# A two-layer hybrid trunk in fp32 on one core: pinned casts of operands, double-width buffers for sums of weights, and norms' sums two blocks later

## The chip, the cores and the metric

The kernel runs on one core of a Trainium2 chip. The metric is the device time of one execution, in microseconds (us). The kernel before took 2816.06, 2812.41 and 2814.46 us in three runs, a median of 2814.46 us. In the trace, PE is the matmul engine (TensorE), DVE is VectorE, ACT is ScalarE, POOL is GpSimd and SP is the engine that issues most of the DMAs; POOL issues the rest.

## The reference

The reference is one inference step of a model with two layers. 1024 prompt positions and 8 single samples share the weights; the width is 1024, the MLP's inner width 4096, and everything is float32. Cut to what matters here:

```python
for l in range(2):
    sh1, s1, g1, sh2, s2, g2 = split(silu(c) @ ada_w[l] + ada_b[l])   # adaLN
    h = rmsnorm(x, norm_mix[l]) * (1 + s1) + sh1
    out = even_mixer(h) if l == 0 else mamba_mixer(h)     # each with its own states
    x = x + g1 * out
    h = rmsnorm(x, norm_mlp[l]) * (1 + s2) + sh2
    x = x + g2 * (square(relu(h @ mlp_w1[l])) @ mlp_w2[l])
y = rmsnorm(x, norm_final)
```

The outputs are y for prompt and samples and the mixers' new states.

## The kernel before

**Layout and matmuls.** x stands transposed on the chip, as 8 tiles of 128 rows (channels) by 1032 columns (1024 prompt positions and 8 samples). A float32 product is made of three matmuls in PE's fast 32-bit format: each operand is cast to a high part on ACT, the low part is the difference to it on DVE, and `mm3` (L484, L487, L488) adds hi·hi, hi·lo and lo·hi. So each unit of weights (128x1024, 512 KB) costs one ACT cast to whi and one DVE subtraction to wlo. whi and wlo have three buffers each, so the cast for a unit waits until PE is through with the unit three before.

**The two MLPs.** Each is done by Strassen's scheme with seven products. The first projection (units "a") runs over 16 pairs of tiles (`AOPS`); `operand` makes the sums of weights there, `kept` fetches back tiles that were written out, `ff_out` applies the activation and stores the sums of activations in DRAM (td). The second projection (units "b", 64 of them in `BOPS`, eight for each of the passes i = 0 to 5 and sixteen half-size ones for i = 6) multiplies weights by operands rr, loaded back from td by POOL's queue in `load_op` (four DMAs of 516 KB for each half operand) and split into a high and a low part by `parts` (ACT's cast L836, DVE's subtraction L837); `split_op` says after which unit a part is split. Passes 2 to 5 need sums of two weights: `prep` loads one summand into h (two tiles of 512 columns, t2 and t3), the other into raw, adds or subtracts them on DVE (L448, L450, L452), casts (L453) and subtracts (L454). The sums of passes 2 and 3 are stored to DRAM (sd) and are the summands of later passes. Passes 0, 1 and 6 use plain weights (L463, L464). `need` prepares three units ahead of PE (AHEAD = 3).

**What runs beside.** While MLP 0's second projection runs, `ada_gen` streams layer 1's adaLN weights in the same loop, four DMAs of 256 KB for a unit into buffers from the same two rings (t2, t3), and PE multiplies them (L316). In the last two passes the norm of the next stage is made in steps, one step after each unit: `to_odd` after MLP 0, `to_out` after MLP 1. Squares are made on ACT (L548, L551) and added on DVE (L552), one matmul with ones sums over the partitions (L520, in `rms`, called by `rstd`); `sample_rstd` does the same for the samples (squares L599, matmuls L602). In the odd mixer `odd_dt` makes decays, writes them to DRAM and reads them back, spread over partitions (o.cd, o.dts).

**What sets the order.** Tiles and their semaphores are placed by a scheduler, which reorders each engine's instructions by its own estimate, except where the kernel keeps an instruction in program order with `tc.keep_in_program_order`. At run time every engine, and SP's DMA queue, takes its instructions in the order written down. SP waits, before it issues a DMA, for the one that it issued eight earlier to land, and for the buffer to be free.

Two lines that the change is about, of `parts` and of `prep`:

```python
S.copy(hi[:, c:c + 2], src)                 # L836: the scheduler places it
h = [t2(512), t3(512)]                      # two tiles, two DMAs, two adds, casts, subtractions
```

Of the kernel before, what the change touches and what calls it, by code (L numbers as in the profile page):

```python
# [32 lines left out]
N2, N3E, N3O, N3M = 8, 14, 6, 8  # L33
# [128 lines left out]
def kernel(ctx: ExitStack, tc: tile.TileContext, A: dict):  # L162
# [29 lines left out]
    def t3(w=W2, dt=F32):  # L192
        t = ph.pool.tile([P, W2], dt, name="t3", tag="t3", bufs=ph.n3)
        return t[:, :w]

# [187 lines left out]
    def operand(l, p, q):  # L383
# [3 lines left out]
        if key not in asrc:  # L387
# [7 lines left out]
            r[5], r[6] = t3(512), t3(512)  # L395
# [4 lines left out]
        if q in (7, 3):  # L400
            a11, a12, a21, s2 = r["a"]
            r[q] = t3(512)
            V.tensor_add(r[q], *((a11, a21) if q == 7 else (a12, s2)))
        return r.pop(q)

    def prep(kind, idx, raw=None, into=None):
# [20 lines left out]
        if kind[0] == "b":  # L427
# [3 lines left out]
            while sums and sums[0][0] <= idx - 2:  # L431
                _, d, h = sums.pop(0)
                for j in range(2):
                    dma(d[:, 512 * j:512 * j + 512], h[j])
            pr = BPROD[i]
            if pr in (5, 6, 7, 3):
# [4 lines left out]
                h = [t2(512), t3(512)]  # L441
                for j in range(2):
                    dma(h[j], a[:, 512 * j:512 * j + 512])
                raw = load_unit(*second)
                for j in range(2):
                    c = slice(512 * j, 512 * j + 512)
                    if pr == 5:
                        V.tensor_add(h[j], h[j], raw[:, c])  # L448
                    elif pr == 3:
                        V.tensor_sub(h[j], raw[:, c], h[j])  # L450
                    else:
                        V.tensor_sub(h[j], h[j], raw[:, c])  # L452
                    S.copy(hi[:, c], h[j])  # L453
                    V.tensor_sub(lo[:, c], h[j], hi[:, c].bitcast(F32))  # L454
# [140 lines left out]
    def sample_rstd(r):  # L595

        q = sm(KT * NS)
        for k in FOURS:
            S.activation(q.rearrange("p (k b) -> p k b", b=NS)[:, k], x[:, k, 512:520], AF.Square)  # L599
        pt = psm()  # L600
        for m in range(KT):
            PE.matmul(pt[:, :NS], ones, q[:, m * NS:m * NS + NS], start=m == 0, stop=m == KT - 1)  # L602
        return newton([(0, NS, pt)], NS, D, r)
# [174 lines left out]
    def mlp(l, gi, finish, more=None):  # L778
# [5 lines left out]
        saved, keep, U, B = {}, {}, {}, {}  # L784
# [41 lines left out]
        def load_op(i, kh):  # L826

            pool, tag = ((big, M["tags"][0]), (ph.pool, "hr"), (big, M["tags"][1]))[BSET[i][kh]]
            hi, lo = R[i, kh] = [pool.tile([P, KT, HX], F32R, name="rr", tag=tag, bufs=2, padded_shape=[P, KT, 520])
                                 for _ in range(2)]  # L830
# [18 lines left out]
        def kept(p):  # L849

            if p in SPLIT and p not in saved:
                saved[p] = t3(HX)
# [3 lines left out]
        for i, (p, q) in enumerate(AOPS):  # L856
# [55 lines left out]
            elif p >= 13 and q in (6, 4):  # L912
# [15 lines left out]
        for n, (i, hb, q, mp) in enumerate(BOPS):  # L928
# [33 lines left out]
            if i == 0:  # L962
                split_op((2, 2, 2, 2, 0, 1, 2, 1)[j])
            else:
                split_op((0, 0, 1, 1, 1, 1, 0, 1)[j] if i == 1 else (2, 1, 1, 1, 1, 1, 0, 1)[j] if i < 6 else (2, 1, 0, 0, 0, 0, 0, 0)[j] if hb == 0 else 0)
# [1133 lines left out]
```

## Time and profile before

| | |
|---|---|
| median of three runs | 2814.46 us |
| the profiled execution | 2808.36 us, its span 2806.4 us |
| PE busy | 2656.0 us, 95% of the span |
| DVE, ACT, POOL busy | 1995.5, 1495.9, 287.5 us |
| moved by DMA | 525.66 MB, 187 GB/s on average |

The stages follow each other: even mixer to 545 us, MLP 0's first projection to 892, its second to 1260, odd mixer to 2102, MLP 1's first projection to 2442, its second to the end. PE is busy nearly all the time, so the profile is read for the places where PE waits: in a list of PE's waits each row has the engine and line that PE waited for, the total, the number of times and the longest. In a timeline, the bracket behind a row gives how long the engine stood idle just before it and what ended that. PE's clock has its own column: 1.00 is 2.4 GHz, 0.50 is 1.2 GHz.

### The profile page before, as it was taken

What the parts mean: (1) busy time and instruction counts of PE and PEld (TensorE: products, weight loads), DVE (VectorE), ACT (ScalarE), POOL (GpSimd) and SP (SyncE); (2) the same over time, 40 slices, a digit from 0 to 9 for tenths busy, and PEclk for the clock granted to TensorE, in tenths of its full rate; (3) what the DMA queues carried; (4) which work ended last, traced back from release to release, by engine and by line L of the source; (5) the groups of instructions that cost most, each with busy time, mean ns of one, the idle gap of its engine ahead of it and who ended that gap; (6) DMA issues with size and microseconds to landing.
All of it is one profiled execution on the core that took longest, in us unless ns stands there. A gap on an engine that the chain in (4) does not pass through costs nothing. (4 is left out here: it accounts for less than half of the span.)

```text
span 2806.4 us, 49697 instructions
## 1 busy us (share of the span) xinstructions
PE 2656.0 (95%) x19442; PEld 2446.8 (87%) x19442; DVE 1995.5 (71%) x3796; ACT 1495.9 (53%) x2473; POOL 287.5 (10%) x492
## 2 busy tenths in 40 slices
PE   6999999999999998999899999999999999999897
PEld 4889888899999887989799897787779999999897
DVE  5666544787757566865799888998778776667766
ACT  5785511463444322446687766878756444444243
POOL 0000000023223111000000000000001322311010
PEclk8999999999999999999899999999999999999999
DMA  8232333256558899834554645543434655879754
GB/s 300 66 105 75 105 107 121 80 183 240 172 196 295 307 375 391 315 128 111 140 163 139 176 142 138 152 130 110 117 118 158 222 182 183 298 290 361 275 173 154
DMA packets 216923, 525.66 MB, mean 187 GB/s; under 512 B 38320, under 2 KB 56112, under 8 KB 216688
## 3 DMA queue, kind: packets, MB, share of 16 engines
q1 hardware_dynamic: 168304, 355.25, 39.7%
q0 software_dynamic: 48384, 167.23, 16.4%
q8 instruction: 153, 2.51, 0.4%
q14 instruction: 82, 0.67, 0.1%
HBM read 408.59 MB, written 113.80 MB: 186 GB/s over the span
## 5 line engine op out<-in xcount | busy, mean ns | idle before, releaser
L484 PE MATMUL pg<-hh,whi 128*128 128x256 f32 (+2 forms) x1616 | 536.7, 332 | 11.0 <-ACT hh L586 5.7
L487 PE MATMUL pg<-hl,whi 128*128 128x256 f32 (+2 forms) x1616 | 524.2, 324 | 1.9 <-DVE hl L587 1.9
L488 PE MATMUL pg<-hh,wlo 128*128 128x256 f32 (+2 forms) x1616 | 523.6, 324 | 0.0
L484 PE MATMUL pd<-rr,whi 128*128 128x258 f32 x1792 | 515.2, 288 | 8.3 <-DVE racc L960 7.2
L488 PE MATMUL pd<-rr,wlo 128*128 128x258 f32 x1792 | 511.2, 285 | 12.3 <-DVE wlo L454 10.5
L487 PE MATMUL pd<-rr,whi 128*128 128x258 f32 x1792 | 510.4, 285 | 0.0
L464 DVE TENSOR_TENSOR wlo<-raw,whi 128x1024 fp32r<-128x1024 f32 x222 | 271.0, 1222 | 199.7 <-ACT whi L463 193.2
L463 ACT CAST whi<-raw 128x1024 fp32r<-128x1024 f32 x222 | 231.4, 1044 | 326.8 <-PE pg L487 203.0
L484 PEld LDWEIGHTS pd<-rr,whi 128*128 128x128 f32 x1792 | 343.4, 192 | 28.2 <-issue 21.7
L488 PEld LDWEIGHTS pd<-rr,wlo 128*128 128x128 f32 x1792 | 343.2, 191 | 15.7 <-DVE wlo L454 11.5
L484 PEld LDWEIGHTS pg<-hh,whi 128*128 128x128 f32 x1616 | 309.1, 191 | 48.0 <-issue 8.7
L487 PEld LDWEIGHTS pd<-rr,whi 128*128 128x128 f32 x1792 | 343.3, 192 | 0.5 <-issue 0.5
L487 PEld LDWEIGHTS pg<-hl,whi 128*128 128x128 f32 x1616 | 309.0, 191 | 30.7 <-issue 5.2
L488 PEld LDWEIGHTS pg<-hh,wlo 128*128 128x128 f32 x1616 | 308.7, 191 | 24.2 <-issue 0.4
L484 PE MATMUL pd<-hh,whi 128*128 128x258 f32 x1024 | 294.2, 288 | 24.2 <-ACT whi L424 10.4
L487 PE MATMUL pd<-hh,whi 128*128 128x258 f32 x1024 | 292.3, 285 | 0.8 <-DVE hh L688 0.8
L488 PE MATMUL pd<-hh,wlo 128*128 128x258 f32 x1024 | 290.6, 284 | 0.0
L484 PEld LDWEIGHTS pd<-hh,whi 128*128 128x128 f32 x1024 | 196.3, 192 | 27.9 <-issue 11.3
L836 ACT CAST rr<-rr 128x1032 fp32r<-128x1032 f32 x112 | 117.8, 1057 | 155.1 <-DMA rr<-td 154.8
L487 PEld LDWEIGHTS pd<-hh,whi 128*128 128x128 f32 x1024 | 196.0, 191 | 1.9 <-DVE hh L688 1.4
L488 PEld LDWEIGHTS pd<-hh,wlo 128*128 128x128 f32 x1024 | 196.1, 192 | 0.0
L837 DVE TENSOR_TENSOR rr<-rr 128x1032 fp32r<-128x1032 f32 x112 | 136.0, 1229 | 65.3 <-ACT rr L836 64.7
(335 smaller groups left out, 5850.4 us busy)
## 6 DMA issues: line engine op xcount, KB each, us to landing
raw<-W SPq DMA_DIRECT2D x375, 512.0 KB, 4.3
td<-x POOLq DMA_DIRECT2D x224, 258.0 KB, 3.9
rr<-td POOLq DMA_DIRECT2D x112, 516.0 KB, 8.4
t<-ada SPq DMA_DIRECT2D x192, 256.0 KB, 5.8
t<-W SPq DMA_DIRECT2D x64, 256.0 KB, 6.6
sd<-t SPq DMA_DIRECT2D x64, 256.0 KB, 5.7
t<-sd SPq DMA_DIRECT2D x64, 256.0 KB, 5.9
t<-csd SPq DMA_DIRECT2D x64, 256.0 KB, 4.6
```

The costliest lines, as they stand in the source:

```text
L463: S.copy(hi, raw)
L464: V.tensor_sub(lo, raw, hi.bitcast(F32))
L484: mm = PE.matmul(pt, wh, xh, start=first and i == 0, stop=False)
L487: PE.matmul(pt, wh, xl, start=False, stop=False)
L488: PE.matmul(pt, wl, xh, start=False, stop=last and i == n - 1)
L836: S.copy(hi[:, c:c + 2], src)
L837: V.tensor_sub(lo[:, c:c + 2], src, hi[:, c:c + 2].bitcast(F32))
```

## The change

Four things change.

1. A ring of four double-width buffers, t6 (2 x 524 columns), takes the place of t3 (eight of 524) in the MLP phases. `operand` and `kept` put two tiles into one; in `prep` h is one tile of 1024 columns: one DMA of 512 KB where there were two of 256 KB, one sum, one cast (L456 of the changed kernel), one subtraction (L457). The adaLN weights use halves of t6 as well.
2. The casts of the operands (L836, now L840) are pinned in ACT's order, and read and write contiguous memory. The table in `split_op`'s calls is changed: the first operand's parts are split during pair 14, not from pair 13 on, and passes 0 and 1 split at other units.
3. `to_odd` and `to_out` make the norm's matmul two steps after the last squares; `sample_rstd` is a generator whose matmuls come two steps after its squares.
4. In `odd_dt` the sample decays are stored so that the four loads of o.dts read rows of 512 bytes, and these loads and that of o.cd move one step later.

```diff
@@ prep
-                h = [t2(512), t3(512)]
-                for j in range(2):
-                    dma(h[j], a[:, 512 * j:512 * j + 512])
+                h = t6()[:, 0:1024]
+                dma(h, a)
                 raw = load_unit(*second)
...
+                S.copy(hi, h)
+                V.tensor_sub(lo, h, hi.bitcast(F32))
@@ sample_rstd
-        q = sm(KT * NS)
+        q = tp.tile([P, KT * NS], F32, name="sq8", tag="racc", bufs=2)
         for k in FOURS:
             S.activation(q.rearrange("p (k b) -> p k b", b=NS)[:, k], x[:, k, 512:520], AF.Square)
+        yield
         pt = psm()
@@ load_op
-                    S.copy(hi[:, c:c + 2], src)
+                    tc.keep_in_program_order(S.copy(hi[:, c:c + 2], src))
@@ first projection
-            elif p >= 13 and q in (6, 4):
+            elif p == NPAIR - 2 and q in (7, 5, 4, 3):
                 split_op()
@@ second projection
             if i == 0:
-                split_op((2, 2, 2, 2, 0, 1, 2, 1)[j])
+                split_op((0, 2, 2, 0, 1, 1, 2, 0)[j])
             else:
-                split_op((0, 0, 1, 1, 1, 1, 0, 1)[j] if i == 1 else (2, 1, 1, 1, 1, 1, 0, 1)[j] if i < 6 else ...
+                split_op((2, 2, 1, 1, 1, 1, 0, 1)[j] if i == 1 else (2, 1, 1, 1, 1, 1, 0, 1)[j] if i < 6 else ...
@@ odd_dt
-            sd = dr.tile([2, 32, NS], F32, name="sd")
+            sd = dr.tile([2, 2, 16, NS], F32, name="sd")
...
-                    dma(o.dts[64 * hh:64 * hh + 64, q], sv[hh:hh + 1].broadcast_to([64, 16, NS]))
...
+                        dma(o.dts[64 * hh:64 * hh + 64, q].rearrange("p m b -> p (m b)"),
+                            sd[q][hh:hh + 1].rearrange("o m b -> o (m b)").broadcast_to([64, 16 * NS]))
@@ to_odd
         state["am1"] = make_amod(1, 1, "nmix")
+        yield
+        yield
         r = t2(520)
         nm.rstd(r[:, :512])
...
-        yield
-        yield
-        sample_rstd(r[:, 512:520])
+        st = sample_rstd(r[:, 512:520])
+        next(st)
+        yield
+        yield
+        next(st, None)
@@ to_out
+        n1.add(0)
+        n1.add(1)
+        yield
+        n1.add(2)
+        n1.add(3)
+        yield
         gen = write(n0, n0.rstd())
...
-        r8 = sample_rstd(sm(NS))
+        r8 = sm(NS)
+        st = sample_rstd(r8)
+        next(st)
+        yield
         yield
         gen = write(n1, n1.rstd())
+        next(st, None)
```

ACT near the end of MLP 0's first projection, in the order before. L424 casts sums and raw weights of the first projection, L795 and L803 are its activations, L836 are the casts of the second projection's first operand:

```order
L424 CAST whi<-t_8300 128x512
L836 CAST rr<-rr 128x2x516 x4
L424 CAST whi<-raw 128x512
L424 CAST whi<-t_8443 128x512
L795 ACTIVATE t_8472<-t_8472 128x516
```

The same stage in the changed kernel, where L431 is the old L424, L799 and L807 the old L795 and L803, and L840 the old L836; these rows stand two pairs later:

```order
L431 CAST whi<-t_8702 128x512
L431 CAST whi<-raw 128x512
L840 CAST rr<-rr 128x1032
L799 ACTIVATE t_8798<-t_8798 128x516
L807 ACTIVATE x<-t_8798 128x516
L840 CAST rr<-rr 128x1032
L431 CAST whi<-t_8629 128x512
L431 CAST whi<-t_8702 128x512
```

The four casts stood together ahead of a weight cast for pair 13; now they stand one by one among weight casts and activations, during pair 14 and later.

ACT in MLP 1's second projection, before. whi numbers grow with the units; rr_28620 is the second half operand of pass 5, rr_28760 the first of pass 6:

```order
L836 CAST rr_28620<-rr_28621 128x2x516 x2
L453 CAST whi_28626<-t2_28628 128x512
L453 CAST whi_28626<-t3_28629 128x512
L836 CAST rr_28620<-rr_28621 128x2x516 x2
L551 ACTIVATE t2_28967<-x_26067 128x512
L453 CAST whi_28688<-t2_28690 128x512
L453 CAST whi_28688<-t3_28691 128x512
L836 CAST rr_28760<-rr_28761 128x2x516
```

The same two operands in the changed kernel, rr_28203 and rr_28333, with L456 the cast of a whole sum and L554 the old L551 (the row ahead of these is the first part of rr_28203):

```order
L840 CAST rr_28203<-rr_28204 128x1032 x2
L456 CAST whi_28404<-t6_28406 128x1024
L840 CAST rr_28203<-rr_28204 128x1032
L456 CAST whi_28466<-t6_28468 128x1024
L840 CAST rr_28333<-rr_28334 128x1032
L554 ACTIVATE t2_28655<-x_25790 128x512
L456 CAST whi_28528<-t6_28530 128x1024
L840 CAST rr_28333<-rr_28334 128x1032
```

Counted in PE's matmuls, the first half of the second operand of pass 5 stood behind the release of a unit four units ahead of its first use; it now stands two units ahead, and the last part one unit ahead of the unit that reads it.

PE in MLP 1's last pass, before. L602 are the samples' sums, the others the product's matmuls:

```order
L487 MATMUL pd<-rr,whi 128x258
L488 MATMUL pd<-rr,wlo 128x258
L602 MATMUL pd<-sm,ones 128x8 x4
L484 MATMUL pd<-rr,whi 128x258
L602 MATMUL pd<-sm,ones 128x8 x4
```

The same place in the changed kernel (L606 is the old L602, L523 the old L520 with the second norm's sum, L487, L490 and L491 the old product):

```order
L490 MATMUL pd<-rr,whi 128x258
L491 MATMUL pd<-rr,wlo 128x258
L523 MATMUL pd<-t_28879,ones 128x254
L606 MATMUL pd<-sq_29162,ones 128x8 x8
L487 MATMUL pd<-rr,whi 128x258
```

Counted from the end of PE's order, the samples' sums stand 49 matmuls later (197 rows from the end before, 147 now, one of them the second norm's sum that now stands ahead); the first norm's sum (L520 of 128x512) moves by two half-size units as well.

## Rows read from the trace of the kernel before

**Rows 1.** Busy time by stage, MLP 0's and MLP 1's second projection: stretch, length, then PE, PEld, DVE, ACT and POOL busy with the number of instructions, PE's clock, share of the DMA engines busy, GB/s.

```profile
892.00:1260.00 368.00, 348.84 (x2791) 323.13 (x2790) 238.68 (x372) 136.80 (x182) 44.90 (x67) 0.98 0.84 308
2442.00:2806.00 364.00, 335.05 (x2714) 332.15 (x2712) 246.77 (x393) 138.08 (x192) 44.35 (x66) 0.97 0.72 255
```

**Rows 2.** PE's waits over the whole span: what PE waited for, total us, times, longest.

```profile
PE pd L484 <- ACT whi L424: 14.6, 4, 5.6
PE pd L488 <- DVE wlo L454: 10.5, 5, 5.8
PE pd L602 <- ACT sm L599: 10.0, 2, 5.0
...
PE pd L484 <- DVE racc L960: 7.2, 3, 2.8
...
PE pd L316 <- DMA t<-ada: 3.4, 3, 2.2
```

**Rows 3.** Timeline of ACT near the end of MLP 0's first projection: start, duration, instruction, idle before it and what ended that.

```profile
838.81 1.06 ACT L836 CAST rr<-rr 128x1032 fp32r<-128x1032 f32 x1 [3.27 <-DMA rr<-td]
...
843.86 0.61 ACT L424 CAST whi<-raw 128x512 fp32r<-128x512 f32 x1
```

**Rows 4.** Timeline of PE, the first matmul behind each of seven waits.

```profile
845.01 0.55 PE L484 MATMUL pd<-hh,whi 128*128 128x258 f32 x1 [4.79 <-ACT whi L424]
2394.81 0.55 PE L484 MATMUL pd<-hh,whi 128*128 128x258 f32 x1 [5.58 <-ACT whi L424]
1220.71 0.67 PE L520 MATMUL pd<-t,ones 128*128 128x512 f32 x1 [1.59 <-DVE t L552]
1246.55 2.30 PE L602 MATMUL pd<-sm,ones 128*128 128x8 f32 x10 [4.91 <-ACT sm L599]
2740.36 0.67 PE L520 MATMUL pd<-t,ones 128*128 128x512 f32 x1 [2.17 <-DVE t L552]
2766.33 1.76 PE L602 MATMUL pd<-sm,ones 128*128 128x8 f32 x8 [5.04 <-ACT sm L599]
1319.18 0.56 PE L484 MATMUL pg<-hh,whi 128*128 128x264 f32 x1 [4.05 <-ACT xy L1434]
```

**Rows 5.** PE in the stretches right behind waits, and in an undisturbed one (the last): stretch, length, busy (number of matmuls), PE's clock, share of the DMA engines, GB/s.

```profile
845.40:848.10 2.70, 2.70 (x14) 0.50 0.13 53
1250.40:1254.40 4.00, 4.00 (x20) 0.50 0.03 10
1319.50:1323.50 4.00, 4.00 (x23) 0.61 0.19 17
2395.20:2397.70 2.50, 2.50 (x13) 0.50 0.14 56
2608.30:2612.80 4.50, 4.50 (x25) 0.63 0.93 319
2646.60:2650.30 3.70, 3.70 (x19) 0.50 0.53 194
2770.20:2773.20 3.00, 3.00 (x15) 0.50 0.15 29
1160.00:1200.00 40.00, 40.00 (x336) 1.00 0.65 238
```

**Rows 6.** Timeline of SP's DMA queue early in the odd mixer: start, time over which the DMAs were issued, DMA, number.

```profile
1302.51 7.44 SPq L217 DMA_DIRECT2D dts<-sd  x4
...
1311.46 0.90 SPq L217 DMA_DIRECT2D t<-csd  x2
```

**Rows 7.** Timeline of ACT at the same place.

```profile
1317.04 0.40 ACT L1520 ACTIVATE t<-t,hs 128x128 f32<-128x128 f32 x1 [7.76 <-DMA t<-csd]
```

**Rows 8.** ACT's waits in MLP 0's second projection, the longest.

```profile
ACT rr L836 <- DMA rr<-td: 77.3, 35, 12.5
```

**Rows 9.** Timeline of ACT in MLP 1's second projection, ahead of a wait of PE.

```profile
2640.98 1.05 ACT L836 CAST rr<-rr 128x1032 fp32r<-128x1032 f32 x1 [1.58 <-DMA rr<-td]
2641.93 1.13 ACT L453 CAST whi<-t 128x512 fp32r<-128x512 f32 x2
```

**Rows 10.** The chain of waits at that place: start, duration, what the time went to.

```profile
2634.24 7.36 DMA t<-sd
...
2645.47 0.61 DVE wlo L454
2646.13 0.58 PE pd L488
```

**Rows 11.** ACT's groups in MLP 0's second projection: line, operation, tile, number, busy us, mean ns, idle before and its releasers.

```profile
L453 ACT CAST whi<-t 128x512 fp32r<-128x512 f32 x64 | 36.8, 618 | 85.9 <-PE pd L487 34.3 <-DVE t L452 23.5 <-issue 7.7
L463 ACT CAST whi<-raw 128x1024 fp32r<-128x1024 f32 x27 | 28.2, 1046 | 42.9 <-PE pd L487 17.1 <-DMA raw<-W 14.9 <-issue 4.6
```

**Rows 12.** DVE's groups in the same stage.

```profile
L837 DVE TENSOR_TENSOR rr<-rr 128x1032 fp32r<-128x1032 f32 x52 | 63.2, 1229 | 33.6 <-ACT rr L836 33.3
...
L464 DVE TENSOR_TENSOR wlo<-raw,whi 128x1024 fp32r<-128x1024 f32 x27 | 33.0, 1221 | 23.3 <-ACT whi L463 23.3
```

**Rows 13.** Busy time in 180 us of each second projection, columns as in rows 1: the stretch in which the adaLN weights are streamed, and one of MLP 1.

```profile
960.00:1140.00 180.00, 169.45 (x1344) 146.70 (x1336) 112.11 (x188) 52.66 (x71) 16.97 (x24) 0.98 1.00 372
2520.00:2700.00 180.00, 169.52 (x1378) 168.49 (x1377) 129.03 (x212) 61.05 (x86) 22.63 (x32) 0.97 0.85 301
```

**Rows 14.** DMAs of the stretch 960 to 1140 us: DMA, queue, number, KB each, median us from issue to landing.

```profile
t<-W SPq DMA_DIRECT2D x32, 256.0 KB, 7.0
```

More of the change, by code (lines that the diff above doesn't have):

```diff
@@ L194, in t3, with t6 @@
         return t[:, :w]
+    def t6():
+        return ph.pool.tile([P, 2 * W2], F32, name="t6", tag="t6", bufs=N6M)
     def sm(w):
@@ L440, in prep @@
                 a = sumd.pop((first[1], q, mp)) if first[0] == "s" else A["W"][WIDX[first]]
-                h = [t2(512), t3(512)]
-                for j in range(2):
-                    dma(h[j], a[:, 512 * j:512 * j + 512])
+                h = t6()[:, 0:1024]
+                dma(h, a)
                 raw = load_unit(*second)
[L445 to L454, printed above, removed]
+                if pr == 5:
+                    V.tensor_add(h, h, raw)
+                elif pr == 3:
+                    V.tensor_sub(h, raw, h)
+                else:
+                    V.tensor_sub(h, h, raw)
+                S.copy(hi, h)
+                V.tensor_sub(lo, h, hi.bitcast(F32))
                 if pr in (5, 6):
@@ L782, in mlp @@
         v2 = lambda a: a.rearrange("p (a t) -> p a t", a=2)
-        saved, keep, U, B = {}, {}, {}, {}
+        saved, keep, U, B, both = {}, {}, {}, {}, [None]
         def slot(p, i):
@@ L828, in load_op @@
             pool, tag = ((big, M["tags"][0]), (ph.pool, "hr"), (big, M["tags"][1]))[BSET[i][kh]]
-            hi, lo = R[i, kh] = [pool.tile([P, KT, HX], F32R, name="rr", tag=tag, bufs=2, padded_shape=[P, KT, 520])
-                                 for _ in range(2)]
+            ts = [pool.tile([P, KT * 520], F32R, name="rr", tag=tag, bufs=2) for _ in range(2)]
+            hi, lo = R[i, kh] = [t[:, 0:KT * HX].rearrange("p (k t) -> p k t", t=HX) for t in ts]
             d = td[BOPND[BPROD[i]]][kh]
@@ L851, in kept @@
             if p in SPLIT and p not in saved:
-                saved[p] = t3(HX)
+                if p % 2 == 0:
+                    both[0] = t6()
+                saved[p] = both[0][:, p % 2 * W2:p % 2 * W2 + HX]
                 dma_aux(saved[p], keep[p])
@@ L1396, in odd_dt @@
         if hf == 0:
-            sd = dr.tile([2, 32, NS], F32, name="sd")
+            sd = dr.tile([2, 2, 16, NS], F32, name="sd")
             es = sm(8)
             act(es, da[:, P:nt], AF.Exp)
-            dma(sd[0], dtt[0:32, P:nt])
-            dma(sd[1], es[0:32])
+            for q, a in enumerate((dtt[0:32, P:nt], es[0:32])):
+                dma(sd[q].rearrange("h m b -> m h b"), a)
             o.dts = ph.pool.tile([P, 2, 16, NS], F32, name="dts")
-            for q in range(2):
-                sv = sd[q].rearrange("(m h) b -> h m b", h=2)
-                for hh in range(2):
-                    dma(o.dts[64 * hh:64 * hh + 64, q], sv[hh:hh + 1].broadcast_to([64, 16, NS]))
         def rest():
             yield
+            if hf == 0:
+                for q in range(2):
+                    for hh in range(2):
+                        dma(o.dts[64 * hh:64 * hh + 64, q].rearrange("p m b -> p (m b)"),
+                            sd[q][hh:hh + 1].rearrange("o m b -> o (m b)").broadcast_to([64, 16 * NS]))
+            dma(o.cd, cdd.rearrange("(o p) a -> o (p a)", o=1).broadcast_to([P, P]))
             yield
@@ L1896 @@
     with ExitStack() as e:
-        phase(e, "mlp0", n3=N3M)
+        phase(e, "mlp0")
         psum(e, "mlp0", 0, 0, 4)
         upto("mlp0")
-        turn = [0]
+        turn, dbl = [0], [None]
         def alloc(w):
             turn[0] += 1
-            return t2(w) if turn[0] % 2 else t3(w)
+            if turn[0] % 4 in (1, 2):
+                return t2(w)
+            if turn[0] % 4 == 3:
+                dbl[0] = t6()
+                return dbl[0][:, 0:w]
+            return dbl[0][:, W2:W2 + w]
         mlp(0, mi(0, 5), to_odd, more=lambda: ada_gen(1, alloc, ((0, 1, 2, 3), (4, 5, 6, 7), (8, 9, 10, 11))))
@@ L1983, in to_out @@
             dma(A["o_y"][k, :, 512:520].rearrange("m p t -> p m t"), ys)
+        next(gen)
         yield
-        for m in range(4):
-            next(gen)
-            if m < 2:
-                n2.add(2 + m)
-            yield
+        next(gen)
+        yield
+        next(gen)
         n2.add(4)
+        n2.add(5)
         yield
-        n2.add(5)
+        next(gen)
         yield
```

26 lines of the change are left out of this document (13 added, 13 removed).

## The prediction

> **What bounds the kernel now.** I read the busy time by stage first: in both second projections PE works 335 to 349 us of 364 to 368, at a clock of 0.97 to 0.98 [rows 1]. So PE sets the end, and the change can only give back time in which PE waits, or in which it runs at half clock behind a wait. Next came PE's waits [rows 2], then each of the larger ones in PE's timeline with what stood ahead of it [rows 4], then the clock behind them [rows 5]. The reader is to see there that a wait of some microseconds costs more than its length: behind it matmuls run at clock 0.50, 14 of them in 2.70 us, while an undisturbed stretch does 336 in 40.00 us, 0.119 us each. The surcharge of a wait is the length of the slow stretch less 0.119 us for each of its matmuls.
>
> The sum is made against the profiled execution, 2808.36 us with a span of 2806.4. It ran 6.1 us under the median of the three runs, 2814.46 us; I take the saving from the median, since new runs will scatter like those.
>
> **1. Operand casts at the end of the first projections.** At 838 us ACT waits for rr<-td, casts four parts (L836) and only then comes to the weight cast L424, at 843.86 [rows 3]; PE waits 4.79 us for it, and 5.58 us at the same place in MLP 1 [rows 4]. In the new order these casts stand two pairs later, behind the weight casts. Two pairs are ten products of 24 matmuls, 240 x 0.119 = 29 us, by when the loads, issued at the same point, have long landed, so both waits go. The slow stretches behind them give 2.70 - 14 x 0.119 = 1.03 and 2.50 - 13 x 0.119 = 0.95 us [rows 5]. Together 4.79 + 5.58 + 1.03 + 0.95 = 12.3 us. The operand is first needed in the next stage, so nothing takes their place; bounds 0 and 12.3, I take 12.3.
>
> **2. Norms' sums.** PE arrives at L520 1.59 and 2.17 us, and at L602 4.91 and 5.04 us, before squares and additions are done [rows 4]. All four matmuls now stand two half-size units later, 2 x 24 x 0.119 = 5.7 us, more than each wait. ACT's squares stay where they were, so the cover holds by 0.7 us in the tightest case. With the clock, 4.00 - 20 x 0.119 = 1.62 and 3.00 - 15 x 0.119 = 1.21 [rows 5], this is 13.71 + 2.83 = 16.5 us. MLP 0's norm has 24 steps, one a unit, and now ends with the eighteenth, so the next stage's start doesn't move. Bounds: 0 to 16.5; I take 16.5.
>
> **3. The odd mixer's spread decays.** The four loads dts<-sd hold SP's queue for 7.44 us, against 0.90 us for the two t<-csd behind them [rows 6]. ACT stands 7.76 us for t<-csd [rows 7], and PE 4.05 us for ACT (L1434) [rows 4]. Rows of 512 bytes instead of 32 make them plain transfers; at 0.45 us each, as the t<-csd, SP reaches t<-csd 5.6 us earlier, which covers PE's wait. With the clock, 4.00 - 23 x 0.119 = 1.26, it is 5.3 us. If the issue time doesn't hang on the row length it is 0. I take 5.3, because the queue's row is the only thing between.
>
> **4. Sums of weights in MLP 1.** PE waits five times for wlo (L454), 10.5 us [rows 2], and the clock behind adds 4.50 - 25 x 0.119 = 1.52 and 3.70 - 19 x 0.119 = 1.44 [rows 5]: 13.5 us at most. Two causes meet there. ACT casts operand parts while their load still lands, part by part, with the weight cast behind each of them [rows 9]; this costs ACT 77.3 us in MLP 0 in 35 waits [rows 8]. By the new order the parts come two to three units (11 to 17 us) later, when they have landed, so this cause goes. The other is the transfer t<-sd that took 7.36 us, ahead of the wait of 5.8 [rows 2, 10]; its bytes stay. I count that wait and its clock (5.8 + 1.44 = 7.2) at half and the rest (6.3) whole: 9.9 us. Bounds 0 and 13.5.
>
> The merged instructions themselves give nothing: one cast of 1024 columns takes 1.05 us where two of 512 take 1.24, on ACT, which idles far longer in this stage [rows 1, 11]. The chain load, sum, cast, subtraction gets longer by it, about 0.7 us, inside a lead of two units.
>
> **5. The adaLN stretch of MLP 0.** PE waits 7.2 us for DVE's racc and 3.4 us for t<-ada [rows 2]. DVE's delay comes from the same operand parts: it stands 33.3 us for L836 [rows 12], and this goes. But all DMA engines are busy there (1.00 at 372 GB/s), while PE works 169.45 of 180 us [rows 13], and the bytes stay the same. So the ends are 10.6 us and, if a lead cut from four units to three starves the queues, a loss (rival c). I take 3 us, nearer to the row that says the queues are full.
> The Trainium skill, "DMA: Bandwidth & Descriptors", section "Bandwidth", says that transfers should be batched to at least 1 MiB, with 64 KB at 32% of peak and 1 MB at 78%; by that the doubled transfers would shorten this stretch, step 5 would be worth its 10.6 us, and the time 2762. The trace disagrees with it as a bound here: 372 GB/s is reached with transfers of 256 KB, many at a time.
>
> **6. What the later casts cost.** The second half operand of each pass now has its last parts cast one unit before use, 48 x 0.119 = 5.7 us. From the release of the unit ahead: weight cast 1.05, operand cast beside wlo's subtraction 1.22, operand's subtraction 1.23, a second one 1.23: 4.7 us [rows 11, 12]. It fits, by 1.0 us. In pass 6 a unit is 24 matmuls, 2.9 us, against 1.05 + 1.22 + 1.23 = 3.5: late by 0.6 us at two parts in each MLP, 4 x 0.6 = 2.4 us. I take a loss of 2.4; bounds 0, and 24 if each of the 12 halves of passes 1 to 6 comes 2 us late (ACT's mean wait, 77.3 / 35 = 2.2 [rows 8]).
>
> **The sum.** 12.3 + 16.5 + 5.3 + 9.9 + 3.0 - 2.4 = 44.6 us. 2814.46 - 44.6 = 2770 us.
>
> **The rivals.**
> a) Everything goes: steps 1 to 3 whole, all of step 4 and step 5's waits, no new ones: 34.1 + 13.5 + 10.6 = 58.2, so 2756 us. For it speaks that one cause, ACT's wait for rr<-td, stands behind most of these; against it the full DMA queues [rows 13].
> b) Only what is far from the sums: steps 1 to 3 give 34.1, steps 4 and 5 nothing, since late transfers set those waits, and step 6 costs 10, between its bounds: 24.1 us, 2790 us. For it speaks the 7.36 us of t<-sd [rows 10].
> c) Slower. The ring of sums now has four buffers where there were eight pairs. SP's queue keeps its order, and a load of h waits until the store of the sum four units ahead has landed and its wlo is made; raw for the next units stands behind that load, and in MLP 0 the adaLN loads too. A load takes 7.0 us there [rows 14], a unit of PE 5.7, so a queue that stands once a unit falls behind over eight units. If each of the eight passes with sums (2 to 5, both MLPs) then costs PE one wait like that at 2646 us, 5.8 with 1.44 of clock [rows 2, 5], that is 8 x 7.2 = 58 us; less the 34.1 of steps 1 to 3, the kernel takes 2838 us. It decides from 34.1 / 8 = 4.3 us a pass. Against it: the loads run three units, 17 us, ahead, and SP issues three DMAs a unit instead of five.
> d) The change doesn't do what it says: the pins keep a waiting operand cast ahead of weight casts, and step 1's kind of wait (4.8 to 5.6 us) turns up in the passes instead, some six times. That takes back 6 x 5.2 = 31 of 44.6 and step 4's gain with it, 2811 us. What would bring it about is that ACT passes nothing by; rows 3 show that in this kernel. Against it: by the order the parts come after the landing.
> The Trainium skill, "TensorE: Matmul & The Clock Gate", section "Architectural detail", calls ACT's and DVE's queues strict FIFO. This speaks against a pin, and by it case d follows whenever a load lands late; the trace agrees, L424 came only behind the fourth L836.
>
> **How the numbers follow.** Forecast 0.50, its own range 2760 to 2780; a 0.14; b 0.18; d, taken as no change, 0.06; c 0.12. Faster by over 0.2% (5.6 us, about what a measurement of this kernel can tell): 0.50 + 0.14 + 0.18 = 0.82; within 0.2%: 0.06; slower 0.12. The range runs from just under a to just above d, 2754 to 2816, and leaves out c and a little of a.
>
> **What would show it.** Right: in the new trace no wait of PE for L424's successor at the end of the first projections, none over 1 us at L520 and L602 apart from the tail's, the four dts loads issued in some 2 us, ACT's waits for rr<-td down from 77 us to under 20, and PE's busy share at clock 1.00 in both second projections. Step 6 shows as waits of PE for the operand's subtraction in pass 6. Wrong: waits for wlo that come back in every pass with SP standing for sd<-t (c), or waits for weight casts behind L840 (d); a DMA share that falls below 0.95 between 960 and 1140 us would make step 5 a loss.

## The result and the profile after

The changed kernel takes 2823.92 us (median of 20 runs, 2817.68 to 2827.88), the kernel before 2813.11 (20 runs, 2805.17 to 2821.71, taken between them). The ratio is 1.0037, its 95% interval 1.0026 to 1.0048: slower by 0.4%, some 10 us. The forecast was 2770, its range 2754 to 2816: the time lies above the range, on the slower side, to which the prediction had given 0.12.

The profiled execution of the changed kernel has a span of 2822.0 us, before 2806.4. First PE's waits over the whole span, which answer to [rows 2] (its helper lines stand 3 to 7 further down now: L484, L488, L454, L837, L424, L890 have become L487, L491, L457, L841, L431, L896):

```profile
PE pd L490 <- DVE rr L841: 32.9, 10, 8.1
PE pd L487 <- DVE t L896: 26.0, 13, 7.2
...
PE pd L320 <- DMA t<-ada: 11.1, 4, 4.5
...
PE pg L487 <- ACT xy L1441: 5.4, 1, 5.4
...
PE pd L523 <- DVE t L555: 1.9, 2, 1.5
```

Three entries of before are gone or nearly: the norms (10.0 at L602 alone, now 0.7), wlo L454 (10.5) and racc (7.2). Two others head the list: the operand's subtraction rr L841 is new, and t L896 has grown from what it was before, in the same list of the kernel before,

```profile
PE pd L484 <- DVE t L890: 8.9, 8, 2.0
```

while t<-ada has grown from 3.4 to 11.1. The second projections, columns as in [rows 1], and the adaLN stretch, as in [rows 13]:

```profile
892.00:1260.00 368.00, 342.28 (x2729) 315.35 (x2728) 224.37 (x286) 125.07 (x136) 35.27 (x67) 0.97 0.84 305
2442.00:2822.00 380.00, 349.91 (x2841) 346.85 (x2839) 254.55 (x345) 142.72 (x174) 39.61 (x75) 0.97 0.72 259
```

```profile
960.00:1140.00 180.00, 160.23 (x1252) 138.38 (x1251) 99.08 (x137) 42.34 (x44) 12.55 (x24) 0.95 0.94 343
```

In the adaLN stretch PE does 1252 matmuls where it did 1344, and the DMA engines are busy 0.94 of the time at 343 GB/s where they were full at 372. So about 11 us (92 x 0.119) go there. Queue by queue, SP's waits in this stretch, of before and of after:

```profile
SPq L217 <- DMA t<-ada: 33.1, 44, 1.8
SPq L217 <- DMA sd<-t: 16.8, 18, 4.4
```

```profile
SPq L221 <- DMA sd<-t: 55.4, 14, 9.1
SPq L221 <- PE pd L320: 32.0, 11, 5.0
```

SP now stands 55.4 us until the store of a sum has landed and a double-width buffer is free, up to 9.1 at a time. One such stand can be followed from SP to PE. Timelines of SP, DVE, ACT and PE at 995 to 1015 us of the changed kernel, behind SP's rows its waits from 995 to 1005.5:

```profile
995.24 0.44 SPq L221 DMA_DIRECT2D raw<-W  x1
1004.87 0.33 SPq L221 DMA_DIRECT2D t<-W  x1
```

```profile
SPq L221 <- DMA sd<-t: 9.1, 1, 9.1
```

```profile
1010.21 1.23 DVE L451 TENSOR_TENSOR t<-t,raw 128x1024 f32<-128x1024 f32 x1 [9.51 <-DMA t<-W]
1011.35 1.22 DVE L457 TENSOR_TENSOR wlo<-t,whi 128x1024 fp32r<-128x1024 f32 x1
1012.49 2.37 DVE L841 TENSOR_TENSOR rr<-rr 128x1032 fp32r<-128x1032 f32 x2
```

```profile
1001.77 2.00 ACT L840 CAST rr<-rr 128x1032 fp32r<-128x1032 f32 x2
...
1011.54 1.05 ACT L456 CAST whi<-t 128x1024 fp32r<-128x1024 f32 x1 [7.29 <-DVE t L451]
```

```profile
1013.77 0.58 PE L490 MATMUL pd<-rr,whi 128*128 128x258 f32 x1 [7.92 <-DVE rr L841]
```

SP is silent from 995.7 to 1004.9, until the store of a sum has landed. The load t<-W is therefore late, and DVE stands 9.51 us for it ahead of the sum L451. The operand's two parts were cast on ACT from 1001.77 on and ready at 1003.8, but their subtractions L841 stand in DVE's order behind that sum and behind L457, and run only from 1012.49. PE needs them and stands 7.92 us; its matmul starts when the first of the two is through (1012.49 + 1.23 = 1013.72). Two parts of the change meet in this chain: the ring makes the sum late, and the new order of the parts has their subtractions behind the sum.

It is so in seven of the ten waits for L841, 31.3 of the 32.9 us: the part's cast had ended 4.8 to 11.5 us before its subtraction began, with a sum and an L457 right ahead of it on DVE, and in six of the seven DVE had just stood idle, 1.6 to 9.5 us, for that sum's load. So the operand was held up on DVE, not by ACT's pinned order itself. Only the casts are pinned; DVE's order is the scheduler's. In passes 2 to 5 the table of `split_op` is the same in both kernels, so there it is the pin, with the contiguous layout, that moved the parts.

At the end of MLP 0's first projection, where step 1 expected no wait, timelines of POOL, DVE, ACT and PE:

```profile
830.89 2.11 POOL L227 DMA_DIRECT2D rr<-td  x4
832.99 1.08 POOL L227 DMA_DIRECT2D t<-kept  x2
```

```profile
842.33 0.69 DVE L896 TENSOR_TENSOR t<-t,pd 128x516 f32<-128x516 f32 x1 [9.39 <-DMA t<-kept]
```

```profile
836.38 0.61 ACT L431 CAST whi<-t 128x512 fp32r<-128x512 f32 x1
```

```profile
843.17 0.55 PE L487 MATMUL pd<-hh,whi 128*128 128x258 f32 x1 [7.23 <-DVE t L896]
```

The weight cast is done at 837, as planned, but PE stands at the same matmul as before (384 matmuls ahead of the first one of the second projection in both traces), and longer (7.23 us against 4.79 in [rows 4]). What it needs now is a bank of PSUM, which DVE frees at L896 when the product kept from earlier has come back from memory; and that copy, t<-kept, stands in POOL's queue behind the four loads rr<-td of the operand.

### The profile page after: what moved, and what is told of

Its sections match the earlier page's. It is cut to its first block, busy times and chain, and to the rows that moved or that the text cites. A ratio compares the mean times of both kernels' runs of the same rounds, so it can differ in the third digit from the quotient of the medians.

```text
span 2822.0 us, 49288 instructions
## 1 busy us (share of the span) xinstructions
PE 2658.2 (94%) x19442; PEld 2446.5 (87%) x19442; DVE 1983.2 (70%) x3668; ACT 1485.2 (53%) x2409; POOL 266.5 (9%) x492
## 5 line engine op out<-in xcount | busy, mean ns | idle before, releaser
L487 PE MATMUL pg<-hh,whi 128*128 128x256 f32 (+2 forms) x1616 | 535.8, 332 | 14.0 <-ACT hh L589 5.7
L490 PE MATMUL pd<-rr,whi 128*128 128x258 f32 x1792 | 513.2, 287 | 33.0 <-DVE rr L841 32.9
L490 PE MATMUL pg<-hl,whi 128*128 128x256 f32 (+2 forms) x1616 | 522.8, 323 | 1.8 <-DVE hl L590 1.8
L491 PE MATMUL pg<-hh,wlo 128*128 128x256 f32 (+2 forms) x1616 | 522.2, 323 | 0.0
L487 PE MATMUL pd<-rr,whi 128*128 128x258 f32 x1792 | 513.9, 287 | 0.0
L491 PE MATMUL pd<-rr,wlo 128*128 128x258 f32 x1792 | 511.3, 285 | 0.0
L490 PEld LDWEIGHTS pd<-rr,whi 128*128 128x128 f32 x1792 | 344.3, 192 | 37.7 <-DVE rr L841 35.6
L487 PEld LDWEIGHTS pd<-rr,whi 128*128 128x128 f32 x1792 | 344.2, 192 | 18.1 <-issue 14.6
L487 PEld LDWEIGHTS pg<-hh,whi 128*128 128x128 f32 x1616 | 308.3, 191 | 51.3 <-ACT whi L466 7.8
L491 PEld LDWEIGHTS pd<-rr,wlo 128*128 128x128 f32 x1792 | 344.8, 192 | 2.6 <-issue 2.5
L490 PEld LDWEIGHTS pg<-hl,whi 128*128 128x128 f32 x1616 | 308.1, 191 | 30.9 <-issue 5.5
L491 PEld LDWEIGHTS pg<-hh,wlo 128*128 128x128 f32 x1616 | 307.6, 190 | 24.0 <-issue 0.4
L487 PE MATMUL pd<-hh,whi 128*128 128x258 f32 x1024 | 295.2, 289 | 30.8 <-DVE t L896 26.0
L490 PE MATMUL pd<-hh,whi 128*128 128x258 f32 x1024 | 293.0, 286 | 0.8 <-DVE hh L692 0.8
L491 PE MATMUL pd<-hh,wlo 128*128 128x258 f32 x1024 | 291.5, 285 | 0.0
L487 PEld LDWEIGHTS pd<-hh,whi 128*128 128x128 f32 x1024 | 197.3, 193 | 34.8 <-issue 28.2
L456 ACT CAST whi<-t 128x1024 fp32r<-128x1024 f32 x64 | 67.1, 1048 | 291.6 <-PE pd L490 120.5
L490 PEld LDWEIGHTS pd<-hh,whi 128*128 128x128 f32 x1024 | 196.8, 192 | 1.9 <-DVE hh L692 1.4
L491 PEld LDWEIGHTS pd<-hh,wlo 128*128 128x128 f32 x1024 | 197.1, 193 | 0.0
L487 PE MATMUL pg<-ffh,whi 128*128 128x264 f32 (+2 forms) x544 | 176.9, 325 | 1.5 <-ACT bcz L1627 0.8
```

What stands on the lines that cost most here:

```text
L456: S.copy(hi, h)
L487: mm = PE.matmul(pt, wh, xh, start=first and i == 0, stop=False)
L490: PE.matmul(pt, wh, xl, start=False, stop=False)
L491: PE.matmul(pt, wl, xh, start=False, stop=last and i == n - 1)
```

## The experiments

All are the kernel before, or the changed kernel, with the edits named. Times are medians; the ratio is to the kernel before on the same chip.

**First: the parts alone.** Two theories were set against each other: P, that the pinned order is the loss, and R, that the ring of four double-width buffers is.

e1, the norms' part alone, at one of its places:

```
-        sample_rstd(r[:, 512:520])
+        st = sample_rstd(r[:, 512:520])
+        next(st)
+        yield
+        yield
+        next(st, None)
```

> Only the third part: norms' sums two steps later. In the changed kernel PE's waits for L520 and L602 did go (0.4 and 0.7 us left, apart from the tail's 1.5), so both theories expect the predicted gain here, 13.7 us of waits and 2.8 of clock: 2797 us against 2813. If it gives less than 8 us, something else takes the place of these waits.

2794.84 us, ratio 0.9950 [0.9931, 0.9968]: 0.50% or 14 us. Step 2 stands.

e2, the ring alone:

```
-N2, N3E, N3O, N3M = 8, 14, 6, 8
+N2, N3E, N3O, N3M, N6M = 8, 14, 6, 8, 4
...
+    def t6():
+
+        return ph.pool.tile([P, 2 * W2], F32, name="t6", tag="t6", bufs=N6M)
...
-                h = [t2(512), t3(512)]
+                h = t6()[:, 0:1024]
```

> Only the first part: the ring of four double-width buffers. Theory P (the loss comes from the pinned casts, which stand too near to their use): same as before, 2805 to 2815 us, no wait of PE for the operand's subtraction. Rival R (the ring of four makes the sums' loads late): slower by 10 to 20 us, 2823 to 2833, with SP waiting some 50 us for sd<-t between 960 and 1140 us.

2823.10 us, 1.0054 [1.0033, 1.0074]: slower by itself, and in R's range. SP's wait for sd<-t and the share of the DMA engines in the adaLN stretch:

```profile
SPq L221 <- DMA sd<-t: 64.0, 15, 8.3
```

```profile
960.00:1140.00 180.00, 159.78 (x1240) 137.44 (x1239) 100.78 (x137) 46.36 (x47) 16.92 (x24) 0.95 0.93 328
```

The starved stretch is there without any pin: 1240 matmuls at 328 GB/s. R holds.

e3, the pinned casts and the table of their places alone:

```
-                    S.copy(hi[:, c:c + 2], src)
+                    tc.keep_in_program_order(S.copy(hi[:, c:c + 2], src))
```

> Only the second part: casts pinned and the table of splits changed, with the old eight and eight buffers for sums. Theory P: slower by 10 to 30 us, 2823 to 2843, with PE waiting some 30 us for the operand's subtraction. Rival R: not slower, 2795 to 2813, since sums arrive as early as before and the short distance is enough.

2813.57 us, 1.0019 [1.0001, 1.0036]: no gain, rather a small loss. That is 9 us under P's range and just above R's, so neither is met. Its waits of PE:

```profile
PE pd L484 <- DVE t L890: 22.0, 10, 6.6
PE pd L487 <- DVE rr L837: 21.7, 6, 6.7
```

Both waits that head the changed kernel's list are here without the ring, so this part brings them by itself: P's mechanism is there, at less than its price. In all six of the waits for L837 the part had been cast 3.2 to 10.0 us before its subtraction began, so DVE's order is behind them here too. The pins, the contiguous layout and the table were not run one by one.

e4, everything but the pinned casts and their table, so the edit of e3 undone in the changed kernel:

```
-                    tc.keep_in_program_order(S.copy(hi[:, c:c + 2], src))
+                    S.copy(hi[:, c:c + 2], src)
```

> The changed kernel with the casts unpinned and the old table of splits; ring, norms and odd mixer as changed. Theory P: the 32.9 us of waits for the operand's subtraction go, 2785 to 2800 us. Rival R: the late sums show up as waits for wlo or for DVE's racc of the same size, 2815 to 2825 us.

2811.80 us, 1.0012 [0.9993, 1.0030], between the two ranges expected. PE has no wait for the operand's subtraction left; 15.9 us for the weight cast L431 stand there again. So the pins and their table cost 0.25% on top of the rest, where the two intervals overlap, and 0.19% alone. The parts nearly add: norms -0.50, ring +0.54, pins +0.19, the odd mixer +0 (e10, below), +0.23% in all against +0.37 measured, within the intervals.

**Second: what each part lacks.**

e5, the changed kernel with the copies of the kept products issued two products earlier, ahead of the operand's loads in POOL's queue:

```
+            if (p, q) == (NPAIR - 2, 2):
+                kept(NPAIR - TAIL)
+                kept(NPAIR - TAIL + 1)
             if (p, q) == FRONT[1][-1]:
                 load_op(0, 0)
```

> The changed kernel with one thing more: the loads t<-kept for pairs 12 and 13 are issued two products earlier, ahead of the four rr<-td in POOL's queue. Theory K (the wait at the end of the first projections moved from the weight cast to t<-kept, which stands behind 2 MB of operand): the waits of 7.2 and 6.7 us for L896 go, with some 2 us of clock: 2806 to 2812 us. Rival: a third cause stands right behind, and the time stays at 2820 or more.

2810.29 us, 0.9997 [0.9987, 1.0007]: 0.40% better than the changed kernel, as the theory had it. POOL's timeline there, and PE's wait for t L896, which was 26.0 with a longest of 7.2:

```profile
824.15 1.07 POOL L227 DMA_DIRECT2D t<-kept  x2
...
830.79 2.11 POOL L227 DMA_DIRECT2D rr<-td  x4
```

```profile
PE pd L487 <- DVE t L896: 13.5, 12, 2.0
```

e6, the changed kernel with all of adaLN's weights in the older single buffers, so that the ring holds sums alone:

```
-            if turn[0] % 4 in (1, 2):
+            if True:
                 return t2(w)
```

> The changed kernel with the adaLN weights loaded into t2 alone, so that the ring of four double buffers is left to the sums. Theory R (sharing the ring of four cuts the lead and lets the DMA queues run dry): SP's wait for sd<-t between 960 and 1140 us falls from 55 to under 25, the DMA share rises from 0.94 to 0.97 or more, PE's wait for t<-ada from 11 to under 5, and the time to 2810 to 2816 us. Rival R2 (four buffers for the sums alone are too few, each waits for its store to land): no change, 2820 to 2828.

2813.02 us, 0.9999 [0.9984, 1.0014]: 0.38% better, as theory R had it. The same two views as for e2:

```profile
SPq L221 <- DMA sd<-t: 6.9, 7, 2.1
```

```profile
960.00:1140.00 180.00, 170.55 (x1373) 148.04 (x1373) 110.96 (x150) 50.31 (x53) 12.53 (x24) 1.00 0.97 371
```

SP's stand falls from 55.4 to 6.9 us, the rate comes back to 371 GB/s, and PE does 1373 matmuls, more than the 1344 before. The ring of four is enough for the sums; it isn't for the sums and adaLN's weights together.

e7, norms and pinned casts without the ring, with three of the operand's parts in passes 1 to 5, casts and subtractions, moved one unit earlier:

```
-split_op(... if i == 1 else (2, 1, 1, 1, 1, 1, 0, 1)[j] if i < 6 else ...
+split_op(... if i == 1 else (1, 0, 1, 1, 1, 1, 0, 3)[j] if i < 6 else ...
```

(The row for i == 1 ends with 3 instead of 1, that for i == 6 begins with 1, 0 instead of 2, 1.)

> Before with the norms' part and the pinned casts, the table of splits changed so that in passes 1 to 5 three parts of the next operand's second half are split at the pass's last unit, not one: their casts run one unit earlier. Theory P (the short distance between cast and use costs): the waits for the operand's subtraction fall from 21.7 us (pinned alone) to under 6, 2780 to 2792 us. Rival (the pins themselves cost, since a part that waits for its load holds the weight casts): as much waiting in another place, 2798 to 2810.

2796.12 us, 0.9943 [0.9928, 0.9958], between the two ranges. The pinned casts now cost nothing beside the norms alone (0.9950), and gain nothing either. PE's waits for the operand's subtraction are 12.6 us, not under 6, one of them 8.3, and 5.15 us of wait for t<-kept are still there at 841 us.

e8, the norms, the copies early as in e5, and the casts of the first operand alone pinned, at the changed kernel's later places:

```
+                    cc = S.copy(hi[:, c:c + 2], src)
+                    if i == 0 and kh == 0:
+                        tc.keep_in_program_order(cc)
...
-            elif p >= 13 and q in (6, 4):
+            elif p == NPAIR - 2 and q in (7, 5, 4, 3):
                 split_op()
```

> Before with the norms' part, the first operand's casts alone pinned and late, and t<-kept ahead of rr<-td. Theory K: both waits at the ends of the first projections (4.0 and 4.9 us in the norms' kernel) go, with 2 us of clock, 2781 to 2787 us. Rival: as for the kept loads in the changed kernel, 2792 or more.

2789.07 us, 0.9915 [0.9898, 0.9932]: 0.35%, 10 us, better than the norms alone, though the two intervals just touch, and 2 us above the theory's range. The counterpart is e11, the norms and the edit of e5, with the casts left as before.

> The kernel before with the norms' part and t<-kept of pairs 12 and 13 issued two products earlier, the casts of the operands left as they were. Theory (two waits, one behind the other; either edit alone gives nothing): as the norms alone, 2793 to 2797, PE waiting 4 to 8 us at the end of each first projection for the cast whi on ACT. Rival (the copies alone were what counted, the casts never did): 2787 to 2791, as with both.

2793.93 us, 0.9939 [0.9919, 0.9959]. The time is the theory's, but the trace isn't: of the waits of 4 to 8 us expected at each end, 1.4 and 1.3 us are there. PE's waits from 780 to 895 us, the end of MLP 0's first projection, in e3 and in e11:

```profile
PE pd L484 <- DVE t L890: 5.4, 1, 5.4
```

```profile
PE pd L484 <- ACT whi L424: 1.4, 1, 1.4
```

At both ends together PE waits 10.4 us in the kernel before, 12.0 in e3 (late casts alone), 8.9 in the norms alone (e1), 2.7 in e11 (early copies) and 0.3 in e8 (both). So late casts by themselves end nothing, early copies by themselves end most of the waits, and both end all. In the times the copies show beside late casts (0.40% in e5, 0.52% in e12 against e7); the times of e11 can't be told from those of e1, nor from those of e8. And e11 isn't quite "the casts as before": the scheduler, free there, put the fourth cast of the operand behind the weight casts.

e13, the changed kernel with nothing but the edit of e7. Its expectation was written with the result of e9, below, known.

> The changed kernel with nothing mended but the positions of the weights' casts in passes 1 to 5 (three parts at the last position, none at the second). Theory (the pinned order's own cost is PE's waits for rr, 51 us in the changed kernel, which a later place of the parts ends): the part of the 49.7 us between the changed kernel and the one with all three mended that the copies (13.6) and adaLN's buffers (11) leave, 25: 2794 to 2804. Rival (the rest comes only when all three are mended together, since the late sums of the adaLN stretch hold the parts wherever they stand): 2810 to 2820.

2798.97 us, 0.9962 [0.9948, 0.9976]: 0.75% better, the largest of the three, and in the theory's range. The edit moves the operand's casts and subtractions, not the weights', and one unit earlier, not later; the 51 us that this expectation and that of e9 name are not in the trace. PE's wait for rr L841 was 32.9 us in 10 times, and is now:

```profile
PE pd L490 <- DVE rr L841: 5.2, 5, 3.9
```

In the adaLN stretch nothing is gained (1257 matmuls at 345 GB/s against 1252 at 343): there the ring holds PE up even when the operand is ready, and the gain comes from elsewhere.

**Third: the odd mixer, and the sum of the mends.**

e10, the norms and the odd mixer's part:

```
-            sd = dr.tile([2, 32, NS], F32, name="sd")
+            sd = dr.tile([2, 2, 16, NS], F32, name="sd")
...
+                            sd[q][hh:hh + 1].rearrange("o m b -> o (m b)").broadcast_to([64, 16 * NS]))
```

> The kernel before with the norms' part and the odd mixer's part alone; beside the norms alone (2794.8). As the prediction had it, the second part is worth 5.3: 2789 to 2790, PE's wait for xy in the odd mixer nearly gone. Theory (what t<-csd gains in being issued earlier its longer landing gives back): 2792 to 2797, and that wait 4 to 6.5 us as in both kernels.

2795.54 us, 0.9947 [0.9931, 0.9963], against 0.9950 for the norms alone, with PE's wait for xy at 4.7 us: the part is worth nothing here, as the theory had it. Its rows are with step 3 below.

e9, the changed kernel with all three mends: the edits of e5, e6 and e7 together.

> The changed kernel with all three mended at once: t<-kept of pairs 12 and 13 issued two products earlier, adaLN's weights in t2 alone (the ring left to the sums), and the weights' casts of passes 1 to 5 moved to positions where their sums are in (three parts at the last position, none at the second). Theory (three separate causes account for the loss): 13.6 from the copies and 11 from adaLN's buffers as each gave alone, and 5 to 15 of the 51 us of PE's waits for rr at L841: 2783 to 2795 us, under the kernel before by 0.5 to 1 per cent, with PE waiting for rr under 20 us. Rival (the causes overlap, or doubling the sums' transfers costs by itself): 2798 to 2812, no better than either mend alone by more than 10.

2774.18 us, 0.9865 [0.9840, 0.9890]: 1.35% faster than the kernel before. The mends alone gave 0.40, 0.38 and 0.75%, together 1.53; all at once give 1.72%, more than the sum by less than the interval. The time is lower than the expectation's lower end by 9 us. Waits of PE, and the adaLN stretch:

```profile
PE pd L487 <- DVE t L896: 14.7, 12, 1.9
...
PE pd L490 <- DVE rr L841: 7.8, 12, 3.9
...
PE pd L320 <- DMA t<-ada: 4.5, 3, 1.9
```

```profile
960.00:1140.00 180.00, 172.64 (x1395) 150.44 (x1394) 113.47 (x155) 51.01 (x53) 12.52 (x24) 1.00 0.97 376
```

All three entries that stood out after the change are down, and PE does 1395 matmuls in the stretch.

e12, the same without the ring and the odd part: the norms, the pinned casts, and the edits of e5 and e7.

> The norms' part, the pinned casts with the parts at the positions of e7, and t<-kept issued two products earlier; no ring, no odd part. Theory (what e7 still waits for at the ends of the first projections is t<-kept, 5.2 us in the one and about as much in the other, and nothing new comes): 2784 to 2790. Rival (the pinned casts' own waits, rr at L838 12.6 us, grow when PE comes earlier): 2791 to 2796, as e7.

2780.05 us, 0.9891 [0.9871, 0.9910]. It is 4 us below its expected range as well. Its interval overlaps that of e9, so what the ring of sums is worth when it isn't shared can't be told from these runs; most of the gain needs neither it nor the odd part.

## Why the prediction was wrong, step by step

**Step 1 (operand casts, 12.3 us): failed.** "By when the loads have landed, so both waits go": the loads had, and the weight cast came in time, but the waits stayed. The step asked what ended the wait and not what would have ended it next. The trace of before had the answer: the timelines of POOL and of DVE show the copies behind the operand's loads, and the subtraction that needs them, already there,

```profile
833.42 2.85 POOL L223 DMA_DIRECT2D rr<-td  x4
836.27 1.09 POOL L223 DMA_DIRECT2D t<-kept  x2
```

```profile
844.18 0.69 DVE L890 TENSOR_TENSOR t<-t,pd 128x516 f32<-128x516 f32 x1
```

and the DMA view of that stretch gives 7.3 us from issue to landing. 836.27 + 7.3 = 843.6; in the changed kernel PE's matmul starts 0.84 us behind the start of this subtraction (842.33 and 843.17 above), so PE could have gone on at 844.4 at the earliest, and did at 845.01: some 0.6 us of 4.79 were to be had from the casts, no more. The bounds had 0 as an end, and the value was taken at the other. With the copies early as well the step is worth 10 us (e8 against e1), near its 12.3; by the waits, most of that is the copies'.

**Step 2 (norms, 16.5): right.** PE's waits at L520 and L602, 13.7 us before without the tail's wait, are 1.1 without it in the changed kernel (2.6 with it), and the part alone gives 0.50% (0.32 to 0.69), 14 us.

**Step 3 (odd mixer, 5.3): failed.** The loads dts<-sd are issued in 2.85 us instead of 7.44, as forecast, but PE still waits 5.4 us for xy. Timelines of SP and ACT in the changed kernel, which answer to [rows 6, 7]:

```profile
1309.53 0.34 SPq L221 DMA_DIRECT2D hs<-cdd  x1
...
1310.44 2.85 SPq L221 DMA_DIRECT2D dts<-sd  x4
...
1313.96 0.91 SPq L221 DMA_DIRECT2D t<-csd  x2
```

```profile
1326.56 0.40 ACT L1527 ACTIVATE t<-t,hs 128x128 f32<-128x128 f32 x1 [9.06 <-DMA t<-csd]
```

The DMA view of these stretches, of before and of after, has for t<-csd:

```profile
t<-csd SPq DMA_DIRECT2D x2, 256.0 KB, 5.7
```

```profile
t<-csd SPq DMA_DIRECT2D x2, 256.0 KB, 12.7
```

In SP's timeline of before hs<-cdd stands at

```profile
1301.59 0.34 SPq L217 DMA_DIRECT2D hs<-cdd  x1
```

Counted from it, t<-csd was issued after 9.9 us (1311.46, [rows 6]) and is now issued after 4.4, so 5.4 earlier; but from issue to landing it takes 7.0 us longer. The step's claim that the queue's row was "the only thing between" was wrong: what counted was the landing, not the issue. ACT's first use of it came 15.5 us behind hs<-cdd before (1317.04) and 17.0 us now (1326.56). The trace of before had one landing of t<-csd at this place, 5.7 us, taken while the queue ahead of it was slow. In e10 it is 11.5 us. Why it takes longer wasn't isolated: the packets of the small transfers ahead are a candidate, and so is the 512 KB load raw<-W, which is issued right ahead of t<-csd in both kernels, 1.5 us before it then and 0.6 us now. In e9, where neither stands right ahead of it, t<-csd lands in 3.4 us and PE's wait for xy is 0.2; no run has only one of the two out of the way.

**Step 4 (sums in MLP 1, 9.9): the waits went, the gain didn't.** PE waits no longer for wlo there. But waits for rr took their place, 18.4 us in five, at 2564, 2572, 2620, 2671 and 2722 us. At 2620 the sum was late by its load, not by SP's stand for a buffer; timelines of ACT, DVE and PE in the changed kernel, and t<-sd in the DMA view from 2600 to 2620:

```profile
2606.84 2.01 ACT L840 CAST rr<-rr 128x1032 fp32r<-128x1032 f32 x2
```

```profile
2617.09 1.22 DVE L455 TENSOR_TENSOR t<-t,raw 128x1024 f32<-128x1024 f32 x1 [2.84 <-DMA t<-sd]
...
2619.36 2.37 DVE L841 TENSOR_TENSOR rr<-rr 128x1032 fp32r<-128x1032 f32 x2
```

```profile
2620.64 0.58 PE L490 MATMUL pd<-rr,whi 128*128 128x258 f32 x1 [8.11 <-DVE rr L841]
```

```profile
t<-sd SPq DMA_DIRECT2D x3, 512.0 KB, 9.0
```

It goes as at 1010 to 1014 above: the casts were done by 2613.6, and the subtractions stood on DVE behind a sum whose load had not landed. The step's "its bytes stay" left out the landing: in 180 us of this stage a t<-sd of 256 KB landed in 5.8 us before, and one of 512 KB takes 7.8 now (medians). ACT's waits for rr<-td are down from 77.3 us ([rows 8], MLP 0) to 6.5, and in MLP 1, which this step is about, from 68.2 to 8.0. So the cause that the step named did go; the place to which the parts went made a new one.

**Step 5 (adaLN stretch, 3.0): wrong sign.** It was a loss, about 11 us by the matmuls above and 0.38% by e6. Rival c had the mechanism, a ring of four that holds up SP's queue, and the prediction's own sign of it, a share below 0.95, is there at 0.94. It was wrong in where: c charged all eight passes at 7.2 us each, 58 us, while a ring that holds sums alone loses nothing in the same stretch (e6, 371 GB/s). That c's 2838 and the measured 2824 both lie on the slower side is in part luck, since steps 1, 3 and 4 failed for other reasons. By the Trainium skill, "DMA: Bandwidth & Descriptors", section "Bandwidth", larger transfers were to raise the rate (its figures are for loads issued from GpSimd, these go by SP and POOL); the runs with the doubled sums show 343 GB/s with the shared ring, and 371 and 376 with one of their own, against 372 before, where transfers of 256 to 516 KB ran side by side. So size moved the rate by nothing that shows here, and the number of free buffers did.

**Step 6 (late casts, a loss of 2.4, bounds 0 and 24): mis-sized, and in another place.** It counted whether the operand's casts and subtractions fit between the release of a unit and their use, and took the sums of weights as punctual. The casts were in time but for two waits of PE of 0.7 us each. The subtractions stand on DVE behind a sum, the sum waits for its load, and so they are as late as the load. The step put its loss into pass 6; none of the ten waits for L841 is there (the last of each MLP, at 1195 and 2723 us, is in pass 5). Moving the parts ahead (e13) gives 0.75%, 21 us: the upper bound, not the lower one, was the nearer. Case d ("the pins keep a waiting operand cast ahead of weight casts") had it the wrong way round and on the wrong engine: PE has no wait for a weight cast in either second projection; a late sum held up the operand on DVE. The rule beside it, that ACT's and DVE's queues are strict FIFO (the Trainium skill, "TensorE: Matmul & The Clock Gate", section "Architectural detail"), agrees with the rows at 1001 to 1012: DVE stands idle for L451 while the subtractions behind it, whose casts are done, don't run.

Taken together: most of the 44.6 us could be had, but steps 1, 4 and 6 each had a condition that the change didn't meet, step 5 a second user of the ring, and step 3 counted an issue where a landing decided. With the first four mended, e9 takes 2774.18, 1.35% or 38 us under the kernel before. The forecast of 2770 lies close to this, but it was for the kernel without the mends, and is wrong for that one.

## What to carry to other kernels

Before counting a wait as gained, look up when the second-latest thing that the waiting instruction needs arrives; the gain is the difference between the two, and for a DMA it can be read as its issue, its landing and what must still run on its data. A pinned order trades one wait for another, and not always on the engine where the pin is: here the casts pinned on ACT were in time, and their subtractions came to stand on DVE behind sums whose loads were late. Follow a moved instruction through every queue that works on its data, and put it only behind instructions whose own inputs are early. When a pool's buffers are doubled in width and halved in number, list all users of the pool; it was the second user, not the one for which the ring was made, that starved the queue.

## What the runs showed that was not expected

Three mends of a few lines each gave 0.40, 0.38 and 0.75%, and nearly added, though two of the three causes stand in one chain.

The clock followed the waits: in the adaLN stretch it is granted 0.95 with the shared ring and 1.00 with the ring left to the sums, so that PE's busy time there, 160.23 against 170.55 us, understates the difference.

In e7, e9, e12 and e13, the four runs with the parts one unit earlier, a wait of 8.5 to 9.8 us appears in the odd mixer that the kernel before has at 2.0 us and no other run above 2.1. PE's waits of e9:

```profile
PE psm L1546 <- DVE mxs L1456: 9.8, 1, 9.8
```

It is the largest single wait left in them beside that at the start; what sets it was not tried.
